# LayerNorm without affine: the first tile's load split over two DMA queues, and the last stores waited for on GpSimd

## Chip, cores and metric

One core of a Trainium2 chip. The metric is device time in microseconds of the slowest core, here the only one. The span of a profile (first to last instruction) is some 1.6 to 1.9 us shorter than the time of the same execution.

## The reference

```python
# x: (32, 512, 1024) float32, eps = 1e-5
mean = np.mean(x, axis=-1, keepdims=True)
var = np.var(x, axis=-1, keepdims=True)
return ((x - mean) / np.sqrt(var + eps)).astype(np.float32)
```

16384 rows of 1024 values: 67.11 MB are read and 67.11 MB written.

## The kernel before

Rows are taken in tiles of 8 x 128 (4 MB); the last 8 x 128 are cut in 6 and 2. A ring of six tile slots in SBUF holds a tile from its load to the end of its store. SP issues all loads, ScalarE all stores. VectorE makes statistics, GpSimd combines them, ScalarE takes the square root and later scales each row in place.

```python
TILES = (8,) * 15 + (6, 2)
SLOT, SLOTS = 8, 6
...
    for t, (K, row, at) in enumerate(plan):              # all loads, on SP
        gone = sorted({owner[r] for r in range(at, at + K) if r in owner})
        ...
        dma = load(nc.sync, t)                           # .then_inc(landed[t], 16)
        if gone:                                         # the slot's tile must be stored
            dma._wait_ge(stored[gone[-1]], sixteens(stored, gone[-1]))
...
    def vector(t, arrived, turn):
        for k in range(K):
            for s in range(NSUB):
                i = nc.vector.bn_stats(...)
                if k == 0 and s == 0:
                    i._wait_ge(landed[t], arrived)
        ...
    for t, (K, row, at) in enumerate(plan):              # ScalarE
        nc.scalar.activation(out=std..., func=AF.Sqrt, ...)
        for k in range(at, at + K):
            i = nc.scalar.activation(out=ring[:, k, :], in_=ring[:, k, :], func=AF.Identity, ...)
        nc.scalar.dma_start(out=rows_of(o2, row, K), in_=ring[:, at : at + K, :]
        )._wait_ge(act, row + K).then_inc(stored[t], 16)

    for t in range(len(plan)):                           # the end
        if t in owner.values():
            nc.sync.wait_ge(stored[t], sixteens(stored, t))
```

Seven tiles are still owners of a slot at the end, so seven waits stand last in SP's stream.

Of the kernel before, what the change touches and what calls it, by code (L numbers as in the profile page):

```python
# [12 lines left out]

FIRST, TURNS = 3, 2

BESIDE = ()


@with_exitstack
def kernel(  # L20
# [6 lines left out]
    nc = tc.nc  # L27
# [3 lines left out]
    x2 = x.flatten_outer_dims()  # L31
    o2 = out.flatten_outer_dims()
# [10 lines left out]
    def sbuf(name, shape):  # L43
        return ctx.enter_context(nc.sbuf_tensor(name, shape, fdt))


    plan, row = [], 0
# [5 lines left out]
    ring = sbuf("ring", [P, SLOT * SLOTS, D])  # L53
# [13 lines left out]
    def places(name):  # L67
        out = [nc.alloc_semaphore(f"{name}_{t}") for t in range(FIRST + SLOTS)]
        for t in range(len(out), len(plan)):
            looped = t < FIRST + TURNS * SLOTS  # L70
            out.append(out[t - SLOTS] if looped else nc.alloc_semaphore(f"{name}_{t}"))
        return out

    def sixteens(sems, t):
        return 16 * sum(1 for s in sems[: t + 1] if s.num == sems[t].num)

    landed, rooted, stored = places("landed"), places("rooted"), places("stored")
    taken, inverse, pool, act = map(
        nc.alloc_semaphore, ("taken", "inverse", "pool", "act")
    )  # L80

    def rows_of(a, row, K):
        return a[row * P : (row + K) * P].rearrange("(p k) d -> p k d", p=P)

    def load(engine, t):
        K, row, at = plan[t]
        return engine.dma_start(  # L87
            out=ring[:, at : at + K, :], in_=rows_of(x2, row, K)
        ).then_inc(landed[t], 16)


    owner = {}
    for t, (K, row, at) in enumerate(plan):
        gone = sorted({owner[r] for r in range(at, at + K) if r in owner})
        owner.update((r, t) for r in range(at, at + K))
        if t in BESIDE:
            assert not gone
            load(nc.scalar, t)
            continue
        for g in gone[:-1]:  # L100
            nc.sync.wait_ge(stored[g], sixteens(stored, g))
        dma = load(nc.sync, t)
        if gone:
            dma._wait_ge(stored[gone[-1]], sixteens(stored, gone[-1]))


    def vector(t, arrived, turn):
        K, row, at = plan[t]
        for k in range(K):
            for s in range(NSUB):  # L110
                i = nc.vector.bn_stats(  # L111
                    out=stats[:, at + k, s, :],
                    in_=ring[:, at + k, s * BN_MAX : (s + 1) * BN_MAX],
                )
                if k == 0 and s == 0:
                    i._wait_ge(landed[t], arrived)
        i.then_inc(taken, 1)
        nc.vector.reciprocal(  # L118
            out=rstd[:, at : at + K], in_=std[:, at : at + K]
        )._wait_ge(rooted[t], turn).then_inc(inverse, 1)  # L120

    nc.vector.memset(eps_t[:], eps_val)  # L122
    for t in range(FIRST):
        vector(t, 16, 1)
# [3 lines left out]
    with nc.vector.Fori(16, 16 * TURNS + 1, 16) as arrived:  # L128
        for t in range(FIRST, FIRST + SLOTS):
            vector(t, nc.vector.lower_val(arrived), turn)  # L130
        nc.vector.reg_add(turn, turn, 1)
    for t in range(FIRST + TURNS * SLOTS, len(plan)):
        vector(t, 16, 1)
# [4 lines left out]
    def gp(i, sem, value):  # L138
        nonlocal npool
        i._wait_ge(sem, value).then_inc(pool, 1)  # L140
        npool += 1
        return pool, npool

    g = nc.gpsimd
    for t, (K, row, at) in enumerate(plan):
        parts = stats[:, at : at + K].rearrange("p g s (h c) -> p g (s h) c", h=2)
        mean4, m2 = parts[:, :, :, 1], parts[:, :, :, 2]
        nm, d, h = nmean[:, at : at + K], dev[:, :K], half[:, :K]
        n = gp(
            g.tensor_tensor(out=h, in0=mean4[:, :, 0:2], in1=mean4[:, :, 2:4], op=ALU.add),  # L150
            taken,
            t + 1,
        )
        n = gp(g.tensor_tensor(out=nm, in0=h[:, :, 0], in1=h[:, :, 1], op=ALU.add), *n)  # L154
        n = gp(
            g.tensor_scalar(out=nm, in0=nm, scalar1=-1.0 / H, scalar2=None, op0=ALU.mult),  # L156
            *n,
        )
        n = gp(
            g.tensor_tensor(  # L160
                out=d, in0=mean4, in1=nm.unsqueeze(2).to_broadcast([P, K, H]), op=ALU.add
            ),
            *n,
        )
        n = gp(g.tensor_mul(out=d, in0=d, in1=d), *n)  # L165
        n = gp(
            g.tensor_scalar(  # L167
                out=d, in0=d, scalar1=float(D // H), scalar2=None, op0=ALU.mult
            ),
            *n,  # L170
        )
        n = gp(g.tensor_tensor(out=d, in0=d, in1=m2, op=ALU.add), *n)  # L172
        n = gp(g.tensor_tensor(out=h, in0=d[:, :, 0:2], in1=d[:, :, 2:4], op=ALU.add), *n)  # L173
# [3 lines left out]
                    out=ss[:, at : at + K], in0=h[:, :, 0], in1=h[:, :, 1], op=ALU.add  # L177
# [7 lines left out]
                    out=nmr[:, at : at + K], in0=nm, in1=rstd[:, at : at + K]  # L185
# [7 lines left out]
    for t, (K, row, at) in enumerate(plan):  # L193
        nc.scalar.activation(  # L194
            out=std[:, at : at + K],
            in_=ss[:, at : at + K],
            func=AF.Sqrt,
            bias=eps_t[:],
            scale=1.0 / D,
        )._wait_ge(*summed[t]).then_inc(rooted[t], 1)  # L200
        for k in range(at, at + K):
            i = nc.scalar.activation(  # L202
                out=ring[:, k, :],
                in_=ring[:, k, :],
                func=AF.Identity,
                bias=nmr[:, k : k + 1],
                scale=rstd[:, k : k + 1],
            ).then_inc(act, 1)
            if k == at:
                i._wait_ge(*ready[t])  # L210
        nc.scalar.dma_start(
            out=rows_of(o2, row, K), in_=ring[:, at : at + K, :]
        )._wait_ge(act, row + K).then_inc(stored[t], 16)


    for t in range(len(plan)):
        if t in owner.values():
            nc.sync.wait_ge(stored[t], sixteens(stored, t))


# [33 lines left out]
```

## Time and profile before

| | before |
|---|---|
| time, median of the 4 runs taken with the changed kernel | 318.05 us (318.02 to 318.42) |
| span of the profiled execution | 316.6 us |
| first tile's load landed | 13.09 us |
| sixteenth increment of the last store | 315.16 us |
| from there to the end of the span ("tail" below) | 1.46 us |

In these traces every DMA has sixteen small semaphore writes (544 for 34 DMAs). I read them as one from each of the 16 DMA engines: the DMA has landed with the sixteenth increment. (The records don't name the engine.) I use one more measure below, from the single packet records: the **excess**, the time that packets took above the ordinary time of their size (1213 ns for 32 KB), summed over a stretch and divided by 16. The lines that show what bounds the kernel are in the prediction.

### The profile page before, as it was taken

What the parts mean: (1) busy time and instruction counts of PE and PEld (TensorE: products, weight loads), DVE (VectorE), ACT (ScalarE), POOL (GpSimd) and SP (SyncE); (2) the same over time, 40 slices, a digit from 0 to 9 for tenths busy, and PEclk for the clock granted to TensorE, in tenths of its full rate; (3) what the DMA queues carried; (4) which work ended last, traced back from release to release, by engine and by line L of the source; (5) the groups of instructions that cost most, each with busy time, mean ns of one, the idle gap of its engine ahead of it and who ended that gap; (6) DMA issues with size and microseconds to landing.
All of it is one profiled execution on the core that took longest, in us unless ns stands there. A gap on an engine that the chain in (4) does not pass through costs nothing.

```text
span 316.6 us, 693 instructions
## 1 busy us (share of the span) xinstructions
DVE 156.8 (50%) x274; ACT 153.0 (48%) x146; POOL 39.3 (12%) x174
## 2 busy tenths in 40 slices
DVE  0387595875290743809347092561916519083000
ACT  1006595775915619074290833808347092567500
POOL 0002202112002020010201102020020200203100
DMA  8999999999999999999999999999999999999995
GB/s 331 397 464 402 426 431 397 461 402 460 423 440 439 422 451 410 455 410 451 410 460 414 447 418 435 418 443 431 439 443 418 447 418 435 431 431 422 455 421 254
DMA packets 4899, 134.24 MB, mean 424 GB/s; under 512 B 544, under 2 KB 544, under 8 KB 544
## 3 DMA queue, kind: packets, MB, share of 16 engines
q1 hardware_dynamic: 2448, 67.11, 49.6%
q10 hardware_dynamic: 2448, 67.11, 49.1%
q14 instruction: 3, 0.02, 0.0%
HBM read 67.11 MB, written 67.11 MB: 424 GB/s over the span
## 4 chain that ended last, share of the span: by engine, by line
DMA 54%; another core or an unknown queue 18%; ACT 9%; DVE 9%; POOL 2%; issue 1%; SPq 0%; ACTq 0%
DMA ring<-in_x_dram 31%; DMA out_dram<-ring 24%; ACT ring L202 9%; DVE stats L111 8%; ACT std L194 0%; SPq L87 0%; POOL dev L167 0%; POOL nmr L184 0%; DVE rstd L118 0%; POOL dev L172 0%; POOL nmean L156 0%; POOL dev L160 0%; POOL dev L165 0%; POOL half L150 0%
## 5 line engine op out<-in xcount | busy, mean ns | idle before, releaser
L111 DVE BATCH_NORM_STATS2 stats<-ring 128x6 f32<-128x512 f32 x256 | 153.5, 678 | 82.2 <-DMA ring<-in_x_dram 81.6
L202 ACT ACTIVATE ring<-ring,nmr,rstd 128x1024 f32<-128x1024 f32 x128 | 146.7, 1227 | 9.3 <-POOL nmr L184 9.3
L194 ACT ACTIVATE std<-ss,eps_t 128x8 f32<-128x8 f32 (+2 forms) x17 | 5.1, 300 | 134.7 <-POOL ss L176 134.3
L150 POOL TENSOR_TENSOR half<-stats 128x16 f32<-128x16 f32 (+2 forms) x17 | 3.9, 231 | 233.0 <-DVE stats L111 233.0
L118 DVE RECIPROCAL rstd<-std 128x8 f32<-128x8 f32 (+2 forms) x17 | 3.4, 200 | 55.4 <-ACT std L194 55.4
L167 POOL TENSOR_SCALAR dev<-dev 128x32 f32<-128x32 f32 (+2 forms) x17 | 5.0, 293 | 1.5
L184 POOL TENSOR_TENSOR nmr<-nmean,rstd 128x8 f32<-128x8 f32 (+2 forms) x17 | 3.5, 203 | 11.9 <-DVE rstd L118 11.9
L172 POOL TENSOR_TENSOR dev<-dev,stats 128x32 f32<-128x32 f32 (+2 forms) x17 | 4.3, 254 | 1.4
L160 POOL TENSOR_TENSOR dev<-stats,nmean 128x32 f32<-128x32 f32 (+2 forms) x17 | 4.1, 239 | 1.4
L165 POOL TENSOR_TENSOR dev<-dev 128x32 f32<-128x32 f32 (+2 forms) x17 | 4.0, 235 | 1.3
L156 POOL TENSOR_SCALAR nmean<-nmean 128x8 f32<-128x8 f32 (+2 forms) x17 | 4.0, 232 | 1.5
L173 POOL TENSOR_TENSOR half<-dev 128x16 f32<-128x16 f32 (+2 forms) x17 | 3.6, 213 | 1.3
L176 POOL TENSOR_TENSOR ss<-half 128x8 f32<-128x8 f32 (+2 forms) x17 | 3.4, 201 | 1.3
L154 POOL TENSOR_TENSOR nmean<-half 128x8 f32<-128x8 f32 (+2 forms) x17 | 3.4, 200 | 1.3
L194 ACT ACT_TABLE_LOAD x1 | 1.3, 1283 | 0.9 <-SPq L52 0.9
L122 DVE MEMSET eps_t<- 128x1 f32 x1 | 0.1, 59 | 1.0 <-SPq L52 1.0
L235 POOL MEMSET const-float32-0.0<- 128x1 f32 x1 | 0.1, 98 | 0.2 <-issue 0.2
L235 POOL MEMSET const-bfloat16-1.0<- 128x1 bf16 x1 | 0.1, 102 | 0.0
L235 POOL MEMSET const-uint8-127<- 128x1 uint8 x1 | 0.1, 101 | 0.0
L235 POOL MEMSET const-float32-1.0<- 128x1 f32 x1 | 0.1, 98 | 0.0
## 6 DMA issues: line engine op xcount, KB each, us to landing
ring<-in_x_dram SPq DMA_DIRECT2D x15, 4096.0 KB, 43.9
out_dram<-ring ACTq DMA_DIRECT2D x15, 4096.0 KB, 48.0
ring<-in_x_dram SPq DMA_DIRECT2D x1, 3072.0 KB, 41.4
out_dram<-ring ACTq DMA_DIRECT2D x1, 3072.0 KB, 18.3
ring<-in_x_dram SPq DMA_DIRECT2D x1, 1024.0 KB, 53.1
out_dram<-ring ACTq DMA_DIRECT2D x1, 1024.0 KB, 17.1
```

What stands on the lines that cost most here:

```text
L111: i = nc.vector.bn_stats(out=stats[:, at + k, s, :], in_=ring[:, at + k, s * BN_MAX : (s + 1) * BN_MAX],)
L118: nc.vector.reciprocal(out=rstd[:, at : at + K], in_=std[:, at : at + K])._wait_ge(rooted[t], turn).then_inc(inverse, 1)
L150: g.tensor_tensor(out=h, in0=mean4[:, :, 0:2], in1=mean4[:, :, 2:4], op=ALU.add),
L156: g.tensor_scalar(out=nm, in0=nm, scalar1=-1.0 / H, scalar2=None, op0=ALU.mult),
L160: g.tensor_tensor(out=d, in0=mean4, in1=nm.unsqueeze(2).to_broadcast([P, K, H]), op=ALU.add),
L165: n = gp(g.tensor_mul(out=d, in0=d, in1=d), *n)
L167: g.tensor_scalar(out=d, in0=d, scalar1=float(D // H), scalar2=None, op0=ALU.mult),
L172: n = gp(g.tensor_tensor(out=d, in0=d, in1=m2, op=ALU.add), *n)
L173: n = gp(g.tensor_tensor(out=h, in0=d[:, :, 0:2], in1=d[:, :, 2:4], op=ALU.add), *n)
L184: g.tensor_mul(out=nmr[:, at : at + K], in0=nm, in1=rstd[:, at : at + K]),
L194: nc.scalar.activation(out=std[:, at : at + K], in_=ss[:, at : at + K], func=AF.Sqrt, bias=eps_t[:], scale=1.0 / D,)._wait_ge(*summed[t]). ...
L202: i = nc.scalar.activation(out=ring[:, k, :], in_=ring[:, k, :], func=AF.Identity, bias=nmr[:, k : k + 1], scale=rstd[:, k : k + 1],).then ...
```

## The change

The intent: VectorE need not wait for the whole first tile, both queues are used from the start, and the last stores are waited for by an engine that has less to do afterwards in the closing barrier. The core of the diff:

```diff
-BESIDE = ()
+HALVES, PARTS = (4, 4), (8,)
...
+    later = nc.alloc_semaphore("landed_later")
+    K, row, at = plan[0]
+    first = 0
+    for n, engine, sem in zip(HALVES, (nc.sync, nc.scalar), (landed[0], later)):
+        engine.dma_start(
+            out=ring[:, at + first : at + first + n, :],
+            in_=rows_of(x2, row, K)[:, first : first + n, :],
+        ).then_inc(sem, 16)
+        first += n
...
                 if k == 0 and s == 0:
                     i._wait_ge(landed[t], arrived)
+                if t == 0 and k == HALVES[0] and s == 0:
+                    i._wait_ge(later, 16)
...
+            if k - at + 1 in ends:
+                n = parts[ends.index(k - at + 1)]
...
     for t in range(len(plan)):
         if t in owner.values():
-            nc.sync.wait_ge(stored[t], sixteens(stored, t))
+            nc.gpsimd.wait_ge(stored[t], sixteens(stored, t))
```

`PARTS` could cut the first tile's store in the same way; with `(8,)` it stays one store.

More of the change, by code (lines that the diff above doesn't have):

```diff
@@ L74, in sixteens @@
     def sixteens(sems, t):
+        if sems is stored and t == 0:
+            return 16 * len(PARTS)
         return 16 * sum(1 for s in sems[: t + 1] if s.num == sems[t].num)
@@ L83, in rows_of @@
         return a[row * P : (row + K) * P].rearrange("(p k) d -> p k d", p=P)
-    def load(engine, t):
-        K, row, at = plan[t]
-        return engine.dma_start(
+    later = nc.alloc_semaphore("landed_later")
[7 more added lines that the diff above has]
+        first += n
+    assert first == K
+    owner = {r: 0 for r in range(K)}
+    for t, (K, row, at) in list(enumerate(plan))[1:]:
+        gone = sorted({owner[r] for r in range(at, at + K) if r in owner})
+        owner.update((r, t) for r in range(at, at + K))
+        for g in gone[:-1]:
+            nc.sync.wait_ge(stored[g], sixteens(stored, g))
+        dma = nc.sync.dma_start(
             out=ring[:, at : at + K, :], in_=rows_of(x2, row, K)
         ).then_inc(landed[t], 16)
-    owner = {}
-    for t, (K, row, at) in enumerate(plan):
-        gone = sorted({owner[r] for r in range(at, at + K) if r in owner})
-        owner.update((r, t) for r in range(at, at + K))
-        if t in BESIDE:
-            assert not gone
-            load(nc.scalar, t)
-            continue
-        for g in gone[:-1]:
-            nc.sync.wait_ge(stored[g], sixteens(stored, g))
-        dma = load(nc.sync, t)
         if gone:
@@ L200 @@
         )._wait_ge(*summed[t]).then_inc(rooted[t], 1)
+        parts = PARTS if t == 0 else (K,)
+        ends = [sum(parts[: i + 1]) for i in range(len(parts))]
         for k in range(at, at + K):
@@ L210 @@
                 i._wait_ge(*ready[t])
-        nc.scalar.dma_start(
-            out=rows_of(o2, row, K), in_=ring[:, at : at + K, :]
-        )._wait_ge(act, row + K).then_inc(stored[t], 16)
+            if k - at + 1 in ends:
+                n = parts[ends.index(k - at + 1)]
+                a = k + 1 - n
+                nc.scalar.dma_start(
+                    out=rows_of(o2, row, K)[:, a - at : a - at + n, :], in_=ring[:, a : a + n, :]
+                )._wait_ge(act, row + k - at + 1).then_inc(stored[t], 16)
     for t in range(len(plan)):
         if t in owner.values():
-            nc.sync.wait_ge(stored[t], sixteens(stored, t))
+            nc.gpsimd.wait_ge(stored[t], sixteens(stored, t))
 _INS = ['x', 'eps']
```

## The prediction

> **What bounds the kernel now.** I read the page first, then the DMA view, then the chain of work that ended last, then stretches of the span side by side, and last the single records at the two ends of the trace, because the change touches only the two ends.
>
> The page's first lines say which resource is full:
>
> ```profile
> span 316.6 us, 693 instructions
> DVE 156.8 (50%) x274; ACT 153.0 (48%) x146; POOL 39.3 (12%) x174
> DMA  8999999999999999999999999999999999999995
> DMA packets 4899, 134.24 MB, mean 424 GB/s; under 512 B 544, under 2 KB 544, under 8 KB 544
> q1 hardware_dynamic: 2448, 67.11, 49.6%
> q10 hardware_dynamic: 2448, 67.11, 49.1%
> ```
>
> No compute engine is busy for more than half of the span. The DMA row is at 9 in every slice but the first and the last. The two queues (q1 carries SP's loads, q10 ACT's stores) take 49.6% and 49.1% of the time of all 16 DMA engines, 98.7% together. So 1.3% of 316.6 us, about 4.1 us, is all that is idle on the DMA engines, and any gain has to come out of that or out of faster packets.
>
> Where these 4 us lie is seen in the busy time by stretches (columns: stretch, its length, DVE, ACT and POOL busy, clock, DMA share, GB/s):
>
> ```profile
> 3.00:14.00 11.00, 0.89 (x2) 0.00 (x0) 0.00 (x0) 1.00 1.00 429
> 14.00:37.00 23.00, 18.37 (x32) 9.46 (x9) 3.33 (x15) 1.00 1.00 433
> 37.00:41.00 4.00, 2.19 (x5) 1.98 (x3) 1.31 (x6) 1.00 0.89 303
> 41.00:288.00 247.00, 132.60 (x231) 131.25 (x126) 32.44 (x140) 1.00 1.00 432
> 288.00:312.00 24.00, 2.64 (x5) 9.07 (x9) 2.07 (x10) 1.00 1.00 429
> 315.20:316.60 1.40, 0.00 (x0) 0.00 (x0) 0.00 (x0) 1.00 0.00 0
> ```
>
> From 3 to 312 us the DMA engines run at 429 to 433 GB/s, but for a dip to 303 GB/s between 37 and 41 us, where the first store joins the loads. After 315.2 us nothing moves. The packet records give the ends closer: the first load packet starts at 1.93 us, the sixteen engines' first packets all end between 3.77 and 4.26 us, the last store packet ends at 314.83 us, and the last of the sixteen increments of the last store arrives at 315.16 us. Following single engines through the records, I find almost no gap between one packet and the next. The middle is bytes over rate, and it doesn't care when the compute engines do their part.
>
> The chain view starts with the first load and shows that what follows is latency hidden behind other transfers:
>
> ```profile
> 0.93 12.16 DMA ring<-in_x_dram
> 13.09 0.02 issue
> 13.11 9.61 DVE stats L111 x16
> ```
>
> ```profile
> 26.44 9.17 ACT ring L202 x8
> 35.62 0.02 issue
> 35.64 25.00 DMA out_dram<-ring
> 60.64 0.02 issue
> 60.65 43.85 DMA ring<-in_x_dram
> ```
>
> The first tile lands at 13.09 us, and VectorE, GpSimd and ScalarE need until 35.6 us for it. But six 4 MB loads are issued without a wait by then, so loads alone keep the DMA engines full all that time (stretch 14 to 37 above).
>
> **What the Trainium skill says.** Four places bear on it.
> "DMA: Bandwidth & Descriptors", section "Issuing engines are not separate DMA queues": transfers issued from several engines run on the same 16 DMA engines and interleave; only sequencer time for issuing is saved. The trace agrees as far as it can: with both queues in use the rate is 432 GB/s, with loads alone 433.
> The same page, section "Queues, rings and completion order": a DMA engine goes round-robin between its queues packet by packet. The trace agrees: after 41 us an engine's packets alternate between q1 and q10.
> The same page, section "Where 436 GB/s comes from": a ceiling of 435.2 GB/s. The trace's 432 to 433 is within 1% of it, so the middle has no rate left to win.
> "Perfetto Trace Analysis", section "DMA Instruction — HWDGE (DVE, Sync)": the descriptor generator is locked for one instruction at a time. The trace only shows SP's own six issues, 0.37 to 0.51 us each; whether ACT's issue will hold up SP's no record here shows.
>
> **The change part by part.**
> *Halves on two queues.* SP's first transfer shrinks from 4 MB to 2 MB, and ACT issues the other 2 MB. Landing time: the two halves share the engines packet by packet, so neither is done early. Each engine has 16 packets of 16 KB for the tile in place of 8 packets of 32 KB, the same bytes; both halves must land near 13 us, as the whole tile did. It would be different with both halves on one queue, where the first half would land some 5 us earlier. So VectorE starts at most about half a microsecond earlier, and the statistics and the first store with it. That is worth nothing in time, as the loads fill that stretch anyway.
> What can count is the first byte. SP issues at 0.93 us; ACT's first instruction now is a table load at 0.89 us, and that slot goes to the load: 0.04 us earlier. SP's descriptors reach the 16 engines between 1.93 and 3.00 us; with two queues each engine takes whichever comes first. But the engines that started early had first packets of 1.4 to 2.2 us in place of 1.213, so effectively all started between 2.56 and 3.05 us. I take 0.1 us off for this part, with 0 to 0.4 as its reach.
> Cost: smaller packets. The records have 1213 ns for 32 KB, 912 for 24 KB and 309 for 8 KB; the last lies 309 − 1213/4 = 5.8 ns above its share, so a fixed cost of about 5.8/0.75 = 8 ns a packet. Eight more packets per engine and one more semaphore write of 9 ns: + 0.07 us. The table load (1.28 us) moves back by about 0.4 us and is over by 2.6 us; its result is needed at 25.6. The extra wait on VectorE is met by then.
> *The first store in parts.* The list of parts holds 8 alone, so tile 0 is still stored by one DMA. Nothing changes.
> *Waiting on GpSimd.* The same seven waits now stand in GpSimd's stream, behind its last arithmetic at 295.4 us. Today's tail, from SP's instructions on the last wait line and on the closing line:
>
> ```profile
> L218 SPq EVENT_SEMAPHORE  x3: 28/28/28, 305.5 to 315.2; - x3
> ```
>
> ```profile
> L52 SPq EVENT_SEMAPHORE  x3: 17/17/28, 315.4 to 315.6; - x3
> L52 SPq NOP  x2: 13/13/13, 0.7 to 315.7; - x2
> L52 POOLq NOP  x1: 13/13/13, 315.4 to 315.4; - x1
> L52 SPq DRAIN  x1: 7/7/7, 315.5 to 315.5; - x1
> ```
>
> In order: SP's last wait is met at 315.176, it branches at 315.241, signals the others at 315.396, GpSimd answers at 315.437, and SP then collects the answers one after the other (315.485, 315.564, 315.617, 315.684) before it joins the barrier at 315.795, which GpSimd takes up at 315.827; 0.77 us later the program is over. After the change SP has signalled and collected all but GpSimd's answer long before. Left is: GpSimd sees the last store (I allow 0.06 us more than SP, as its instructions in this trace start 0.07 us after their releaser against 0.02 on VectorE and ScalarE), about 315.22; the second wait and branch 0.08 us; the jump to the next block 0.155 us as on SP; its answer at 315.46; SP's collecting instruction at 315.50, its two drains at 315.55 and 315.61, the barrier taken up at about 315.65. That is 0.17 us before 315.827; I take 0.15.
> *Sum.* −0.10 + 0.07 − 0.15 = −0.18 us, so 317.84 us from 318.02.
>
> **The rivals.**
> *A ring's first use costs time, and it is moved to where it's hidden.* At 37.7 to 41 us, just after q10's first issue at 35.64, every engine has one or two load packets of 1.3 to 2.1 us; per engine some 0.6 to 0.85 us is lost. The first load packets lose up to 0.7 us in the same way. If that is the price of waking a queue for the first time, ACT's early load pays it while the engines are not yet running, and up to 0.7 us is gained: 317.2. Against it: q10 falls empty again from about 13 to 35.6 us, and if an empty queue, or the first writes to memory among reads, is the cause, the loss comes back in full. I give it one in five; for that I move my number to 317.7.
> *The lock or the double stream costs more than it saves.* If both issues hold each other up, SP's later loads are issued some 0.4 us later. They have 9 us of transfers ahead of them, so no harm; only the very first packets can be late, by 0.3 us: about 318.2.
> *GpSimd is slow at the end.* Its waits could take 0.1 us each more than SP's. Only the last wait and the branch count, the others being met earlier: + 0.2 us, 318.2.
> *The first tile lands early and the pipeline gains microseconds.* This is the apparent intent. Against it are the shared engines and the full DMA row: even an early first store only changes the order of transfers. It would show as 313 to 315; I give it 2%.
>
> **Range and chances.** Two per cent are 6.4 us, more than all the idle time there is on the DMA engines (4.1 us), so faster by 2% is next to impossible, and slower by 2% would need a stall that no record points to. Runs before lie within 0.06 us of each other, so the range holds my doubts on the parts alone: from 317.1 (the first rival in full, on top of the tail) to 318.2 (second or third).
>
> **What would show it.** Right: VectorE's first statistics begin between 12.5 and 13.2 us; first packets at 1.85 to 1.95 us; the rate in the middle stays 429 to 433 GB/s; the stretch from the last store's landing to the end shrinks from 1.4 to about 1.25 us; the dip at 37 to 41 us stays near 303 GB/s. The first rival is right if that dip is gone. The prediction is wrong if the first half lands near 7 us, if the tail is longer than before, or if the sum of idle DMA time changes by more than 1 us.

## The result

| | before | after |
|---|---|---|
| median of 4 runs | 318.05 us (318.02 to 318.42) | 317.90 us (317.75 to 318.41) |
| ratio, 95% interval | | 0.9996 (0.9978 to 1.0013) |
| span of the profiled execution | 316.6 us | 315.9 us |
| first tile landed, both halves | 13.09 us | 13.46 us |
| sixteenth increment of the last store | 315.16 us | 314.69 us |
| tail from there | 1.46 us | 1.24 us |

A ratio is the mean time of one kernel's fast runs over that of the other's of the same rounds, so it isn't quite the ratio of the medians. The result is "the same": the interval is wider than any effect in it.

The page of the changed kernel:

```profile
span 315.9 us, 694 instructions
DMA  7999999999999999999999999999999999999996
DMA packets 5043, 134.24 MB, mean 425 GB/s; under 512 B 560, under 2 KB 560, under 8 KB 560
q10 hardware_dynamic: 2592, 69.21, 51.0%
q1 hardware_dynamic: 2448, 65.01, 47.9%
```

ScalarE's queue q10 has 2.1 MB more, SP's q1 as much less: the moved half. The two shares sum to 98.9%, before 98.7%. The packets are 144 more: 128 from the halving and 16 from one more set of semaphore writes.

Busy time by stretches, after (the same columns as in the prediction):

```profile
3.00:14.00 11.00, 0.52 (x1) 0.00 (x0) 0.00 (x0) 1.00 1.04 444
37.00:41.00 4.00, 1.83 (x4) 1.61 (x3) 1.60 (x7) 1.00 0.94 344
41.00:288.00 247.00, 132.98 (x232) 131.62 (x126) 32.45 (x140) 1.00 1.00 433
288.00:312.00 24.00, 2.64 (x5) 9.06 (x9) 2.06 (x10) 1.00 0.99 426
```

The middle is what it was. The dip at 37 to 41 us looks milder, 344 GB/s against 303, but that is mostly an artefact of a short window, as the view counts a packet's bytes where it starts: from 37.5 to 41.5 us the kernel before has 393 GB/s. Over 36 to 44 us both kernels move 393 GB/s. The excess there is 0.62 us after and 0.76 before; more on this below.

The beginning of the chain of work that ended last in that part of the span, after:

```profile
0.93 12.53 DMA ring<-in_x_dram
13.46 0.02 issue
13.48 9.61 DVE stats L115 x16
```

VectorE waits for the first half until 13.46 us, 0.37 us longer than it waited for the whole tile: the half isn't early at all. The other half, on ScalarE's queue, had landed at 13.28 us.

The end, from the instructions on the last wait line and the closing line, after:

```profile
L229 POOLq EVENT_SEMAPHORE  x3: 42/43/43, 305.0 to 314.7; - x3
...
L52 SPq NOP  x2: 13/13/13, 0.7 to 315.0; - x2
...
L52 POOLq COMPARE_BRANCH  x1: 33/33/33, 314.8 to 314.8; - x1
L52 POOLq NOP  x1: 13/13/13, 315.0 to 315.0; - x1
```

The waits are on GpSimd now. Its last one is met at 314.713 us, 0.02 us after the increment; it branches at 314.800, answers at 314.961, SP sees that at 315.001 and the barrier is taken up at 315.144. From the last increment to the barrier this is 0.45 us, before 0.67. The spans differ by 0.7 us; 0.22 of that is this tail, and the other 0.47 is the moment of the last increment. The experiments show that the latter scatters from trace to trace.

### The profile page after: what moved, and what is told of

The parts are those of the page before. It is cut to its first block, busy times and chain, and to the rows that moved or that the text cites. A ratio compares the mean times of both kernels' runs of the same rounds, so it can differ in the third digit from the quotient of the medians.

```text
span 315.9 us, 694 instructions
## 1 busy us (share of the span) xinstructions
DVE 156.8 (50%) x274; ACT 153.0 (48%) x146; POOL 39.3 (12%) x174
## 4 chain that ended last, share of the span: by engine, by line
DMA 61%; DVE 18%; ACT 9%; POOL 4%; issue 2%; ACTq 0%; DVEq 0%; SPq 0%
DMA ring<-in_x_dram 31%; DMA out_dram<-ring 29%; DVE stats L115 17%; ACT ring L210 9%; ACT std L200 1%; POOL dev L173 1%; POOL dev L178 1%; POOL dev L166 0%; POOL dev L171 0%; POOL nmean L162 0%; POOL half L156 0%; POOL half L179 0%; POOL ss L182 0%; DVE rstd L124 0%; POOL nmean L160 0%
## 6 DMA issues: line engine op xcount, KB each, us to landing
ring<-in_x_dram SPq DMA_DIRECT2D x1, 2048.0 KB, 12.5
```

## The experiments

Each run of an experiment was timed against the kernel before on the same chip; the medians of the kernel before were 317.95 us (first four runs), 318.04 (next four) and 318.05 (last four).

### 1. The changed kernel again

No edit.

> The changed kernel as it is, once more, against the kernel before, because four runs spread over 0.66 us cannot show 0.2 us. My theory (both ends of a DMA-bound program: the halves are worth nothing, waiting on GpSimd is worth 0.2 us): ratio 0.9990 to 0.9997, the stretch from the last store's last increment to the end 1.24 us against 1.46 us before. Rival (the halves matter, by an earlier first byte or a ring woken early): ratio 0.998 or lower. Rival (chance alone): ratio within 0.0002 of 1.

Measured: 317.91 us, ratio 0.9998 (0.9985 to 1.0011). Tail 1.24 us, last increment at 314.98 us. So five rounds don't resolve the effect either. The traces do: an end of 1.24 us is repeated to the hundredth, while the last increment came 0.29 us later than in the first trace of the same kernel. By its ratio the run fits the theory of chance best; that the tail is really shorter is seen only in the trace.

### 2. The waits on GpSimd alone

```diff
-            nc.sync.wait_ge(stored[t], sixteens(stored, t))
+            nc.gpsimd.wait_ge(stored[t], sixteens(stored, t))
```

> The kernel before with only the last waits moved to GpSimd. My theory: the tail after the last increment is 1.22 to 1.27 us instead of 1.46, all else as before, time 0.15 to 0.25 us below before (ratio about 0.9993). Rival (the gain, if any, is in the halves): the tail shrinks in the trace but the time stays within 0.05 us of before, or the tail doesn't shrink without the halves.

Measured: 317.76 us, ratio 0.9995 (0.9982 to 1.0008); tail 1.24 us. The shorter tail belongs to this part of the change alone and doesn't need the halves.

### 3. The halves alone

The changed kernel with this part undone:

```diff
-            nc.gpsimd.wait_ge(stored[t], sixteens(stored, t))
+            nc.sync.wait_ge(stored[t], sixteens(stored, t))
```

> The changed kernel with the last waits back on SP. My theory: tail 1.46 us again; first tile complete at about 13.4 us (later than 13.09, because the startup cost is paid on two queues); the slow packets between 36 and 44 us cost about 0.6 us an engine against 0.76 before; time within 0.1 us of before. Rival (the halves matter): ratio 0.9990 or lower. Rival (they harm): ratio above 1.0005.

Measured: 317.80 us, ratio 0.9997 (0.9984 to 1.0010); tail 1.46 us again; first half landed at 13.38 us; excess between 36 and 44 us 0.62 us. The halves leave the tail alone and give no effect that the rounds could show.

### 4. Both halves on SP: the first half really early

```diff
-    for n, engine, sem in zip(HALVES, (nc.sync, nc.scalar), (landed[0], later)):
+    for n, engine, sem in zip(HALVES, (nc.sync, nc.sync), (landed[0], later)):
```

> The changed kernel, but with both halves issued by SP. Both theories of the round robin agree that the first half then lands near 7.8 us and the second near 13.1. My theory: VectorE starts 5 us earlier and ScalarE's first store is issued earlier (about 30 us, its bound being the second half), yet the time stays within 0.15 us of the changed kernel, as the DMA engines are full either way. Rival (the latency of the first tile counts, as the change intends): time 2 to 5 us lower. It also shows whether the slow packets near 38 us follow the first store: then they move forward to about 33 us.

Measured: 322.63 us (320.10 to 323.32), ratio 1.0138 (1.0111 to 1.0165). The mechanics came out as expected: the first half landed at 8.19 us, the second at 13.06, VectorE began at 8.2 us and the first store was issued at 30.85 us. The time did not: it's 1.4% **slower**, with an interval clear of 1. Both theories missed this.

The trace is of an execution of 320.10 us, the quickest of the six; four others took 322.3 to 323.3 us and were not profiled. So it shows where about 2 us go, and not the whole loss of the median. Busy time by stretches at the end, first before, then in this run:

```profile
314.00:316.00 2.00, 0.00 (x0) 0.00 (x0) 0.00 (x0) 1.00 0.02 8
```

```profile
314.00:316.00 2.00, 0.00 (x0) 0.00 (x0) 0.00 (x0) 1.00 0.24 102
```

Before, next to nothing moves after 314 us. Here the DMA share is still 0.24: four of the sixteen DMA engines are late. Twelve gave their increment of the last store within 1.35 us of the first; the other four came 2.0, 3.1, 3.3 and 3.4 us after it. The sixteen increments of the loads lie 0.4 us apart at 32 us, 1.8 at 50, 3.0 at 108 and 4.6 at 263 us, so these engines fall behind step by step. In the tail-only run the spread stays between 1.8 and 2.7 us from 46 us on. The packet records show what the time is lost in: after 44 us the slow run has 63 packets that take over 50 ns more than their ordinary time, 51 of them loads, scattered from 53 to 266 us; the tail-only run has 3.

### 5. The same, but VectorE waits for both halves

```diff
+        if t == 0:
+            nc.vector.wait_ge(later, 16)
         for k in range(K):
...
-                if t == 0 and k == HALVES[0] and s == 0:
-                    i._wait_ge(later, 16)
```

> Both halves of the first tile on SP, as in the run that came out 1.4% slower, but VectorE begins only when both have landed, so the first store goes out at 35.7 us as in the kernel before. Theory A (the early start moves the stores against the loads, and that makes a few DMA engines fall behind): ratio within 0.001 of 1, and the sixteen increments of the late loads lie within 2.7 us of each other as before, not 4.6. Theory B (two transfers on one queue, or SP's extra issue, are what costs): ratio near 1.014 again, with the increments 4.6 us apart.

Measured: 317.99 us, ratio 0.9998 (0.9985 to 1.0011); first store issued at 35.79 us; increments of the late loads within 1.4 us. Theory A holds against B here: two transfers on one queue cost nothing that shows, VectorE's early start costs 1.4%.

### 6. The first tile 9.7 us late

In the kernel before:

```diff
+        if t == 0:
+            nc.vector.wait_ge(landed[1], 16)
         for k in range(K):
```

> The kernel before, but VectorE doesn't begin the first tile until the second one has landed too, 9.7 us later than needed; the first store goes out near 45 us. My theory (the latency of the first tile is hidden behind six prefetched loads): time within 0.3 us of before, ratio within 0.001 of 1, although everything on the compute engines starts 9.7 us later. Rival (the first tile's latency counts one to one): about 327 us, ratio 1.03. If the order of loads and stores matters by itself, as the slow run hints, some other ratio up to 1.01, with the engines' increments spread more widely or less.

Measured: 317.84 us, ratio 0.9996 (0.9982 to 1.0009), with the first store at 45.54 us in place of 35.64. Nearly ten microseconds of delay at the start of the compute chain leave no mark on the time. This is the direct proof that the latency the halves aim at is hidden. The late loads' increments lie within 1.4 us. The slow packets went along with the first store: excess 0.00 us between 36 and 44, and 0.89 between 44 and 100 us, nearly all of it at 47 to 51 us.

### 7. The store queue used first by a load

In the kernel before:

```diff
-BESIDE = ()
+BESIDE = (5,)
...
-            load(nc.scalar, t)
+            load(nc.scalar, t)._wait_ge(landed[0], 16)
```

> The kernel before, with the sixth tile's load moved to ACT's queue and issued when the first tile has landed (13.1 us), so that this queue is used first by a load among loads, and the first store comes later. Theory 1 (waking an idle queue costs about 0.7 us an engine): slow packets near 15 us, and fewer or none when the first store joins near 38 us. Theory 2 (the first stores among loads cost it): no slow packets near 15 us, about 0.6 to 0.8 us of excess near 38 us as before. Time within 0.5 us of before unless the order of transfers matters by itself.

Measured: 317.68 us, ratio 0.9993 (0.9974 to 1.0011). Busy time by stretches, this run:

```profile
13.00:18.00 5.00, 4.68 (x8) 1.28 (x1) 0.00 (x0) 1.00 0.97 419
36.00:44.00 8.00, 2.89 (x6) 1.87 (x3) 2.32 (x10) 1.00 1.01 393
```

From 13 to 18 us the kernel before has the same 419 GB/s, and the load's first packets on the second queue, at 17.2 us, have no excess. From 36 to 44 us there is the same dip to 393 GB/s and an excess of 0.80 us. So the dip comes with the first store among loads, not with waking a queue, and an early load cannot move it.

### 8. Only the last store waited for on GpSimd

In the kernel before:

```diff
-            nc.sync.wait_ge(stored[t], sixteens(stored, t))
+            (nc.gpsimd if t == len(plan) - 1 else nc.sync).wait_ge(
+                stored[t], sixteens(stored, t)
+            )
```

> The kernel before, with the last store alone waited for on GpSimd and the six others on SP. My theory of the tail (what counts is the chain of single instructions behind the last increment): one wait instruction of about 0.09 us less on GpSimd than with all waits there, so 1.15 us from the last increment to the end, against 1.24 with all on GpSimd and 1.46 on SP. Rival (it is GpSimd's place in the barrier that saves the time, whatever it waits for): 1.24 us again. Time about 0.3 us below before, which the rounds can hardly show.

Measured: 317.68 us (317.52 to 317.76), ratio 0.9987 (0.9974 to 1.0000); tail 1.15 us. The closing line's instructions on GpSimd, this run:

```profile
L52 POOLq COMPARE_BRANCH  x1: 33/33/33, 314.9 to 314.9; - x1
L52 POOLq NOP  x1: 13/13/13, 315.1 to 315.1; - x1
```

With all waits on GpSimd, the last store's wait (314.713 us) stands one instruction before the branch (314.800 us): in the trace the seven waits are three instructions of two waits each and the branch, which carries the odd one. Here the branch itself waits for the last store: 0.09 us less, as expected.

### 9. Parts of six and two rows on SP

Experiment 4 with another cut:

```diff
-HALVES, PARTS = (4, 4), (8,)
+HALVES, PARTS = (6, 2), (8,)
```

> Both parts of the first tile on SP, as six rows and two in place of four and four, VectorE beginning with the first part: it should begin near 10.4 us and the first store go out near 33.2 us, between the slow run's 30.9 and the usual 35.7. Theory A (the earlier the first store, the further some DMA engines fall behind): a ratio between 1.002 and 1.012 and a spread of the late loads' sixteen increments between 2.7 and 4.6 us. Rival (only a particular coincidence, a load issued half a microsecond after a store in every period, does it): no loss, ratio within 0.001 of 1, where the two issues are further apart.

Measured: 318.15 us, ratio 1.0002 (0.9989 to 1.0015); first store at 33.42 us; late loads' increments within 2.8 us. No loss, although the spread of the increments is in theory A's forecast range: the harm doesn't grow evenly with an earlier start, and theory A in its plain form is wrong.

### 10. The first tile stored in two parts

The changed kernel with the knob that it has for this:

```diff
-HALVES, PARTS = (4, 4), (8,)
+HALVES, PARTS = (4, 4), (4, 4)
```

> The changed kernel, but the first tile stored in two parts of four rows, which its code allows for: the first store goes out near 31.3 us, while the statistics of all tiles stay where they are. If it is the early first store by itself that lets engines fall behind, this run is slow too (ratio 1.01); if it is the shift of the whole tile pipeline behind it (VectorE's early start), this run stays within 0.001 of 1. Either way the slow packets near 38 us should move to about 34 us with the first store, if the first store is what makes them.

Measured: 317.94 us, ratio 0.9995 (0.9982 to 1.0007). Last store's increments within 1.2 us. So an early first store by itself doesn't make engines fall behind. And the slow packets come early with it. Busy time by stretches, first before, then this run:

```profile
30.00:37.00 7.00, 5.58 (x10) 5.61 (x5) 1.01 (x5) 1.00 1.04 449
36.00:44.00 8.00, 5.19 (x10) 4.97 (x6) 2.06 (x9) 1.00 1.00 393
```

```profile
30.00:37.00 7.00, 5.75 (x10) 5.88 (x6) 0.92 (x4) 1.00 1.05 412
36.00:44.00 8.00, 5.02 (x10) 5.10 (x6) 2.17 (x10) 1.00 1.01 434
```

The dip is in the first stretch here and in the second before. Together with experiments 6 and 7 this settles what it comes with: the first store. How the store does it stays open. The slow packets are loads: in the kernel before there are 29 between 37.7 and 41.1 us, and 21 of them start before the first store packet does at 39.67 us, though after the store's issue at 35.64.

### 11. The changed kernel with experiment 8's tail

```diff
-            nc.gpsimd.wait_ge(stored[t], sixteens(stored, t))
+            (nc.gpsimd if t == len(plan) - 1 else nc.sync).wait_ge(
+                stored[t], sixteens(stored, t)
+            )
```

> The changed kernel with only the last store waited for on GpSimd, the others on SP: 1.15 us from the last increment to the end, as in the run of the kernel before with that tail. My theory that the halves are worth nothing: the same ratio as that run within noise, 0.9985 to 0.9995. Rival (halves add something): 0.998 or lower.

Measured: 317.72 us (317.52 to 317.85), ratio 0.9990 (0.9977 to 1.0003); tail 1.15 us. The halves add nothing to experiment 8. These two have the lowest means of all versions against the kernel before, but neither interval excludes equality.

### 12. All loads in halves

In the kernel before, with VectorE waiting for 32 in place of 16 on each tile:

```diff
-        return engine.dma_start(
-            out=ring[:, at : at + K, :], in_=rows_of(x2, row, K)
-        ).then_inc(landed[t], 16)
+        return [
+            engine.dma_start(
+                out=ring[:, at + n : at + n + K // 2, :],
+                in_=rows_of(x2, row, K)[:, n : n + K // 2, :],
+            ).then_inc(landed[t], 16)
+            for n in (0, K // 2)
+        ][0]
```

> The kernel before, every load as two transfers of half the rows on SP, VectorE waiting for both: packets of 16 KB in place of 32 KB for all loads, twice as many. My estimate of 8 ns a packet from the records makes 128 more packets per engine and 17 more semaphore writes: 1.03 + 0.15 = 1.2 us, ratio 1.0037, all in the nominal packet time. If smaller packets cost nothing, ratio within 0.001 of 1; if the queue itself is hurt by twice the issues (0.33 us each on SP, which idles), more than 1.006.

Measured: 328.30 us (326.65 to 329.84), ratio 1.0314 (1.0285 to 1.0342). The term I meant to measure is about right: the packets' ordinary times sum to 312.32 us an engine against 310.96 before, 1.36 us for 1.2 expected. But the loss is 10 us, and it's of another kind. If each engine takes a packet of the one queue and then one of the other, then with 16 KB loads against 32 KB stores the stores get two thirds of the rate while both queues have work. The records agree: from 41 to 65 us they have 139 GB/s of loads and 289 of stores here, 201 and 228 before; and the reverse in experiment 10, whose first tile is stored in 16 KB packets among loads of 32 KB: 283 of loads and 142 of stores. The landings show it too: the first stores land at 55.2, 70.4, 85.0 and 99.6 us, 15 us apart, where the kernel before has 60.6, 80.0, 99.3 and 118.7, 19 us apart. So the loads fall behind, and at the end the store queue has run dry. Busy time by stretches, this run:

```profile
298.00:304.00 6.00, 4.39 (x8) 6.00 (x6) 1.14 (x5) 1.00 0.14 59
```

The third tile from the end was complete only at 282.1 us (259.6 before). The DMA engines stood nearly idle from 300.9 us, when the store before it had landed, until it had gone through the compute engines and its own store was issued at 304.7 us. The last load landed at 302.3 us (288.7 before). There is also an excess of 5.8 us in all (1.6 before), and the loads' increments lie up to 13.5 us apart; how much of this, and of the loss, has its cause in the unequal packets, and how much in twice the number of issues (the expectation's own rival), was not tested. SP's own issue took 3.6 to 4.2 us each for its last three of the twelve that need no wait.

### Summary of the traces

| Run | waits on | tail, us | last increment, us | first store issued, us | excess, total, us |
|---|---|---|---|---|---|
| before | SP | 1.46 | 315.16 | 35.64 | 1.61 |
| after | GpSimd | 1.24 | 314.69 | 36.00 | 1.56 |
| 2 waits alone | GpSimd | 1.24 | 315.00 | 35.72 | 1.57 |
| 3 halves alone | SP | 1.46 | 314.76 | 35.94 | 1.51 |
| 4 both on SP | GpSimd | 1.24 | 317.04 | 30.85 | 2.21 |
| 6 first tile late | SP | 1.46 | 314.78 | 45.54 | 1.65 |
| 8 last wait alone | SP, GpSimd | 1.15 | 314.89 | 35.72 | 1.73 |
| 11 changed, last alone | SP, GpSimd | 1.15 | 314.77 | 35.84 | 1.44 |

The runs left out of the table fit it: the tail is 1.24 us with all waits on GpSimd (1 again, 5, 9, 10) and 1.46 us with all on SP (7, 12). In these traces the tail depends on who waits for what, and on nothing else in the change. The last increment scatters by half a microsecond without a visible regard to the change; the 315.16 of the first trace is the highest among these but for the slow run, and part of it, 0.23 us of excess at 190 to 200 us, occurs in no other trace of this table but the slow run's, where it is 0.04.

## Why the prediction was right

The time lies in the range (317.9 us in 317.1 to 318.2), and the class was the one forecast. That the number is so near is luck. The "0.06 us" between earlier runs understated the scatter: the four runs of the kernel before that were timed with the changed one lie 0.40 us apart, the eleven timed with experiments 5 to 8 lie 1.44 us apart, and the effect that the steps add up to is 0.18 us. The summed steps gave 317.84 us, nearer than the 317.7, which is within this noise too. What can be judged is the class and, from the traces, the steps; they fared like this.

**The bound.** Right, and shown directly: 9.7 us of delay for the first tile changed nothing (experiment 6), because loads fill the DMA engines meanwhile.

**"neither is done early".** Right about both halves, in one respect too kind: they landed 0.2 to 0.4 us *later* than the whole tile, at 13.28 and 13.46 us, outside my window of 12.5 to 13.2 us for VectorE's start. In the five traces with halves on two queues the tile is complete at 13.38 to 13.55 us and SP's half at 13.24 to 13.55; in the five with a whole first tile, at 13.09 to 13.29. So the sign "12.5 to 13.2 us" failed, while the reason given, that both halves share the engines, is what the trace shows. It agrees with the Trainium skill, "DMA: Bandwidth & Descriptors", section "Issuing engines are not separate DMA queues".

**"I take 0.1 us off" for the first byte.** Wrong. The first packet starts at 1.934 us in both kernels, though ScalarE issued at 0.89 us. The first sixteen packets start on average at 2.09 us against 2.30 in these two traces, but that is mostly scatter: the mean over the five traces with halves on two queues is 2.15 us (2.09 to 2.24), and over five with a whole first tile 2.18 (2.11 to 2.30). And an earlier start is paid back by slower first packets: that start and the excess up to 10 us come together to 2.84 to 2.91 us in the first five and 2.83 to 2.92 in the others. The step failed in taking an issue that is 0.04 us earlier for an earlier start of useful work.

**Smaller packets, + 0.07 us.** Right: 16 KB packets take 611 ns, the ordinary times sum to 311.04 us against 310.96, + 0.08. But experiment 12 shows that a packet's size does more when the other queue has another size: it shifts the rate from loads to stores. The change escapes that, as both halves have the same size and only the first tile is cut.

**Waiting on GpSimd, − 0.15 us.** Right in mechanism, a third too small: 0.22 us, in every trace. I had allowed GpSimd 0.06 us more than SP for seeing the increment; it needed 0.02 us, like SP. My allowance came from its arithmetic instructions, which start 0.07 us after their releaser.

**The rival of the ring's first use.** Its claim, that an early load takes the loss away, is refuted by experiments 6, 7 and 10: the slow packets come with the first store. Its sign, the dip of 303 GB/s, was a poor one, as it hangs on where the window starts. Something is left over, though. In the five traces with halves on two queues the excess at the first store is 0.61 to 0.67 us, in four with a whole first tile and the usual time of the first store 0.76 to 0.80. That is steady, but it isn't the queue's earlier use as such, since experiment 7 had a load on this queue until 37.3 us and is one of the four; its cause is open. The packets' extra 0.08 us eat half of it, and the times show no gain. So the 0.14 us that I moved my number for were not earned by the reason given.

**The rivals of the lock and of a slow GpSimd.** Neither showed. ScalarE's issue at 0.89 us took 0.39 us, and SP's second issue is at 1.35 us in both kernels, its sixth at 3.43 us against 3.36. GpSimd's tail is shorter, not longer.

**The rival that an early first tile gains.** Rightly given little, and then it surprised: where the first half truly comes early (experiment 4), the kernel gets 1.4% slower. Shown is that VectorE's early start is needed for it (experiment 5), that an early first store is not enough (10), and that a start half as early does no harm (9). Not settled is what makes four DMA engines fall behind. One thing sets the slow run apart. From the timeline, the issues around 113 us in it, then before:

```profile
113.43 0.34 ACTq L222 DMA_DIRECT2D out_dram<-ring  x1
113.95 0.33 SPq L104 DMA_DIRECT2D ring<-in_x_dram  x1
```

```profile
107.68 0.34 ACTq L211 DMA_DIRECT2D out_dram<-ring  x1
118.70 0.33 SPq L87 DMA_DIRECT2D ring<-in_x_dram  x1
```

In the slow run a load and a store are issued half a microsecond apart here, and within 0.7 us of each other in every period from 94 to 231 us; in the kernel before they are 8 to 11 us apart, in experiment 9 about 4.4 us, and in experiment 10 about 1.6 us (102.59 and 104.20 us), without loss. This is a coincidence that fits, not a cause that was tested.

**Readings that were off.** The program ended 0.79 us after GpSimd took up the barrier, not 0.77, and the first load packets lose up to 0.98 us by the prediction's own figures (2.19 against 1.213), not 0.7. No step rests on either.

## What to carry to other kernels

When the DMA row is full from the first microseconds to the last and several tiles are prefetched, don't spend effort on the latency of the first tile before a test: delay it on purpose once, and if the time stays, that latency is free. What could still be gained here was between the last increment and the end, and there one counts single instructions (0.3 us at best in the traces, too little for these timings to confirm); let the last semaphore be waited for alone, as the last thing, by an engine whose answer the closing barrier needs anyway. Mind that unequal packet sizes shift the rate between two busy queues (experiments 10 and 12), and when a cut for latency makes a kernel slower, compare how far apart the sixteen increments of one DMA lie.

## What the Trainium skill lacked or had wrong

- "DMA: Bandwidth & Descriptors", "Queues, rings and completion order", has the round robin by packet but not what follows for unequal packets: with 16 KB loads against 32 KB stores the stores had 289 GB/s and the loads 139 from 41 to 65 us (experiment 12), with the sizes the other way round 142 and 283 (experiment 10).
- The same page, "Latency and other measured facts", gives about 600 ns to the first byte for transfers issued by SP or ScalarE. Here the first packet started 1.0 us after the first issue (0.93 to 1.93 us). A transfer that joined busy DMA engines took longer: 4.0 us for the first store (35.64 to 39.67 us), and 3.9 us for the load on the second queue in experiment 7 (13.31 to 17.16 us).
- None of the pages that I read has the cost of the first stores among loads: 0.6 to 0.9 us of excess per engine, wherever the first store is put.
- None of them says that the sixteen engines can drift apart when nothing but the times of issues differs: increments of one load 4.6 us apart in experiment 4, against 1.1 to 2.9 us in the runs of normal speed.
- No page that I read gives the number of issues that SP can have open: in experiment 12 its tenth, eleventh and twelfth took 3.6, 4.2 and 4.2 us, the nine before 0.37 to 0.53 us.
